# Rows of the last expert unit through a weighted one-hot product, and the overflow loop in the middle of the expert stage

## The chip, the core and the metric

The kernel runs on one core of a Trainium2 chip. Five engines work beside each other, each through its own list of instructions in order: TensorE (PE, matrix products into PSUM), VectorE (DVE), ScalarE (ACT), GpSimd (POOL) and SyncE (SP, which here issues most of the DMAs). They wait for each other by semaphores. The metric is the device time in us of one execution. Three runs of the kernel before took 1588.84 to 1589.75 us, median 1589.25 us.

## The reference

Two layers of a transformer over 512 tokens of width 1024, all in fp32. Each layer is a token mixer with four branches, which the change doesn't touch, and a mixture of experts with a residual and a layer norm:

```python
for l in range(DEPTH):
    mix = _token_mixer(x, ...)
    x = _layernorm(alpha * x + mix, ln1_g[l], ln1_b[l])
    ffn = _hier_moe(x, ...)
    x = _layernorm(alpha * x + ffn, ln2_g[l], ln2_b[l])
...
def expert_block(args):
    xe, e = args
    hid = jax.nn.silu(xe @ w_gate[e]) * (xe @ w_up[e])
    return hid @ w_down[e]
...
y = jnp.einsum('tkd,tk->td', y_assign.reshape(n_tok, TOP_K, d), weights)
```

A router sends each token to 2 of 32 experts, so there are 1024 pairs of a token and an expert (slots). Each expert has 2 MB of gate and up weights and 1 MB of down weights.

## The kernel before

The function `moe` runs the experts of a layer, `combine` adds their rows to the residual and applies the layer norm. The first four experts are taken in their own order, the others by falling number of tokens. They form 18 units of 128 rows: units 0 and 1 with two of the first experts each, units 2, 6, 10 and 14 with one expert of 128 rows, all others with two experts of 64 rows. Rows of an expert beyond these places are left to a loop (`tc.For_i` at L1604) whose number of rounds is computed on the chip; with these inputs it makes none.

A stream (`est`, class `Stream`, L201) brings the weights in loads of 1 MB: for each unit the gate and up weights of its experts, then the down weights of the unit before. A wide unit has 3 loads, a pair 6, a layer 96. SP issues a load as soon as its buffer is free and the DMA lane that it shares with the load eight places earlier has been served; 13 loads are kept ahead of the use.

For each unit u the steps are: `window` (its token columns copied out of `xs` by DVE and ACT), `gemm` (four pieces of gate and up products), `hidden` (ACT and DVE), `hidden_t` (two transposes and a copy), `down` (the down products, two evictions into a tile `ob`, one by ACT and one by DVE, and a `scatter` by POOL of the 128 rows to their slots in `ys_dram`). The code is written so that the gemm of unit u+1 stands between hidden and down of unit u. All of this is in a manual schedule: each engine gets its instructions in the order in which the code is written.

After unit 17, ACT multiplies the residual `x1` (two tiles, four times 128 tokens) by alpha. Then comes the loop, and behind it `combine`: SP loads from `ys_dram`, for each of four tiles of 128 tokens, the two rows of each token (`y`, L1698). ACT loads the table with the square root (L1694). In layer 0, ACT and DVE split two loads of the next layer's weights (`nxt`) into a high and a low part. For each tile `add` (L1644) then makes x = w1·y0 + x and x = w2·y1 + x on DVE, `stats` finds mean and variance (on ACT, or on DVE for tile 0 of layer 0 and tile 3 of layer 1) and `affine` normalizes. In layer 1 the result is stored; in layer 0 it is transposed and goes straight into the next layer's first products.

## Time and profile before

| | us |
|---|---|
| median of three runs | 1589.25 |
| the profiled execution | 1587.72 |
| its span, from the first to the last instruction | 1585.8 |
| TensorE busy in the span | 1466.5 |
| DVE busy | 719.8 |
| ACT busy | 563.2 |
| mean DMA rate over the span | 205 GB/s |

Busy times are those of instructions; the ends of matmuls are modelled, so a busy TensorE is not one at its peak. The profile page cuts the span into 40 slices of about 40 us. A timeline's row gives start and duration in us, engine (PEld is TensorE's weight load; q is an engine's sequencer, which issues DMAs), line of the kernel, operation, what it writes and reads, a count where equal instructions were merged, and in brackets how long the engine was idle before and what ended that.

### The profile page before, as it was taken

The numbers are of one execution on the slowest core, as the hardware profiler recorded it, in microseconds if no ns is written. First come the engines' busy times: TensorE is split into PE (matmuls) and PEld (weight loads), VectorE is DVE, ScalarE is ACT, GpSimd is POOL, SyncE is SP. The second block draws the span as 40 slices with busy tenths as digits, with TensorE's granted clock in tenths as the row PEclk, the third lists the DMA queues.
The fourth block names the chain that finished last, engine by engine and source line by source line (L and its number), as shares of the span: only waits on it lengthen the run. The fifth ranks groups of instructions, "written<-read, shape, count | busy, mean of one in ns | idle before, by whom it ended". The sixth has DMA issues, their size and how long they took to land. (4 is left out here: it accounts for less than half of the span.)

```text
span 1585.8 us, 17859 instructions
## 1 busy us (share of the span) xinstructions
PE 1466.5 (92%) x6552; PEld 939.5 (59%) x6552; DVE 719.8 (45%) x1386; ACT 563.2 (36%) x1001; POOL 138.4 (9%) x121
## 2 busy tenths in 40 slices
PE   7999999999999999988399999999999989999980
PEld 6766787788887433322197666767888874333220
DVE  7558875434455411110465578764443554111005
ACT  6666435333322211111346664353333222111113
POOL 0000000121004200000000000001110141000000
PEclk9999999999998999999799999999999999999996
DMA  5111122122247899999721121211232669999994
GB/s 216 66 67 67 54 93 87 47 100 93 98 193 278 346 419 421 420 420 415 302 87 54 60 93 54 100 67 67 72 121 80 248 234 397 419 421 420 420 399 174
DMA packets 54043, 324.59 MB, mean 205 GB/s; under 512 B 8641, under 2 KB 9281, under 8 KB 21953
## 3 DMA queue, kind: packets, MB, share of 16 engines
q1 hardware_dynamic: 44880, 299.54, 47.6%
q0 software_dynamic: 9072, 23.89, 4.0%
q8 instruction: 52, 0.85, 0.2%
q14 instruction: 39, 0.31, 0.1%
HBM read 306.62 MB, written 27.26 MB: 211 GB/s over the span
## 5 line engine op out<-in xcount | busy, mean ns | idle before, releaser
L149 PE MATMUL ps_mm<-xh,wh 128*128 128x512 f32 (+1 forms) x768 | 309.0, 403 | 8.7 <-ACT xh L128 8.1
L150 PE MATMUL ps_mm<-xl,wh 128*128 128x512 f32 (+1 forms) x768 | 303.4, 395 | 0.0
L151 PE MATMUL ps_mm<-xh,wl 128*128 128x512 f32 (+1 forms) x768 | 302.6, 394 | 0.0
L1451 PE MATMUL ps_mm<-er,xw 128*64 128x512 f32 (+1 forms) x1024 | 289.2, 601 | 10.4 <-DMA er<-in_w_gu_dram 7.0
L162 DVE TENSOR_TENSOR wl<-raw,wh 128x1280 fp32r<-128x1280 f32 (+2 forms) x116 | 169.7, 1467 | 146.0 <-ACT wh L128 145.7
L1451 PEld LDWEIGHTS ps_mm<-er,xw 128*64 128x64 f32 (+1 forms) x1024 | 89.5, 144 | 176.6 <-issue 142.0
L128 ACT ACTIVATE wh<-raw 128x1280 fp32r<-128x1280 f32 (+2 forms) x116 | 135.1, 1168 | 140.3 <-PE ps_mm L150 99.9
L149 PEld LDWEIGHTS ps_mm<-xh,wh 128*128 128x128 f32 (+1 forms) x768 | 144.2, 188 | 50.4 <-issue 10.1
L151 PEld LDWEIGHTS ps_mm<-xh,wl 128*128 128x128 f32 (+1 forms) x768 | 143.8, 187 | 33.8 <-issue 3.1
L1489 PE MATMUL ps_s<-er,ht 128*64 128x512 f32 (+1 forms) x512 | 144.1, 599 | 20.2 <-DMA er<-in_w_dn_dram 13.3
L150 PEld LDWEIGHTS ps_mm<-xl,wh 128*128 128x128 f32 (+1 forms) x768 | 144.2, 188 | 31.2 <-issue 2.0
L1459 DVE TENSOR_TENSOR sg<-sg,ps_mm 128x256 f32<-128x256 f32 x36 | 15.1, 420 | 256.8 <-ACT sg L128 256.8
L1489 PEld LDWEIGHTS ps_s<-er,ht 128*64 128x64 f32 (+1 forms) x512 | 44.0, 143 | 109.8 <-issue 76.3
L415 POOL TENSOR_TENSOR macc<-macc,sg 128x512 f32<-128x512 f32 x32 | 43.0, 1345 | 697.1 <-PE ps_mm L150 498.6
L128 ACT ACTIVATE sg<-ps_mm,par 128x512 f32<-128x512 f32 x64 | 44.1, 688 | 139.1 <-PE ps_mm L151 139.1
L705 DVE SCALAR_TENSOR_TENSOR cacc<-cvh,par,cacc 128x512 f32<-128x512 f32 x120 | 89.5, 746 | 1.7
L1473 DVE COPY ob<-ps_s 128x512 f32<-128x512 f32 x36 | 24.9, 692 | 132.0 <-PE ps_s L1489 132.0
L414 DVE SCALAR_TENSOR_TENSOR sg<-sg,ps_p 128x512 f32<-128x512 f32 x48 | 33.0, 687 | 105.3 <-PE ps_p L151 97.8
L1478 POOL DMA_INDIRECT ys_dram<-ob,rowi x36 | 35.2, 977 | 418.1 <-DVE xw L1439 307.6
L128 ACT ACTIVATE ht<-ps_t 128x256 f32<-128x256 f32 x36 | 13.8, 384 | 159.4 <-PE ps_t L1466 159.4
L128 ACT ACTIVATE sg<-ps_mm 128x256 f32<-128x256 f32 x36 | 13.8, 383 | 139.6 <-PE ps_mm L1451 139.6
L149 PE MATMUL ps_p<-yh,wh 128*128 128x512 f32 x128 | 51.2, 400 | 0.0
(410 smaller groups left out, 2029.1 us busy)
## 6 DMA issues: line engine op xcount, KB each, us to landing
er<-in_w_gu_dram SPq DMA_DIRECT2D x128, 1024.0 KB, 20.5
er<-in_w_dn_dram SPq DMA_DIRECT2D x64, 1024.0 KB, 20.6
raw<-in_wg_dram SPq DMA_DIRECT2D x32, 1280.0 KB, 5.5
raw<-in_wz_dram SPq DMA_DIRECT2D x12, 1024.0 KB, 4.8
raw<-in_w_o_dram SPq DMA_DIRECT2D x8, 1024.0 KB, 4.8
y<-ys_dram SPq DMA_DIRECT2D x8, 1024.0 KB, 10.1
x_dram<-r POOLq DMA_DIRECT2D x8, 512.0 KB, 3.8
x<-x_dram SPq DMA_DIRECT2D x4, 1024.0 KB, 16.8
```

Of the source, the lines that this page charges most:

```text
L128: inst = ACT.activation(out_, in_, func, **kw)
L149: PE.matmul(o, x.h, y.h, start=start, stop=False)
L150: PE.matmul(o, x.h, y.l, start=False, stop=False)
L151: PE.matmul(o, x.l, y.h, start=False, stop=stop)
L162: DVE.tensor_tensor(l, src, h, op=OP.subtract)
L414: DVE.scalar_tensor_tensor(sg, sg, 1.0, p2, op0=OP.add, op1=OP.mult)
L415: (DVE if n == 2 else POOL).tensor_tensor(macc[:, d], macc[:, d], sg, op=OP.add)
L705: DVE.scalar_tensor_tensor(cacc[c], cvh[c][:, j:j + S], w, cacc[c], op0=OP.mult, op1=OP.add)
L1451: PE.matmul(s_["p"][h], s_["X"][:, k, h], w[:, k % 4], start=k == 0, stop=k == KD - 1, skip_group_check=True)
L1473: DVE.tensor_copy(ob[:, 512:], p)
L1478: POOL.indirect_dma_start(out=ys_dram[:, :], out_offset=bass.IndirectOffsetOnAxis(ap=idx, axis=0), in_=ob, in_offset=None, bounds_check=SL ...
L1489: PE.matmul(p[h], s_["ht"][:, c, h], w[:, c, hf * 512:(hf + 1) * 512], start=c == 0, stop=c == 1, skip_group_check=True)
```

## The change

Four things change.

1. The loop for overflowing experts, now `beyond()`, stands between units 8 and 9 (`PAUSE`), outside the manual schedule. Its loads are issued by POOL and no longer by SP. The units are run by `run(2, 9)` and `run(9, 18)`, so unit 9's gemm no longer stands between hidden and down of unit 8, and unit 8's down weights come ahead of unit 9's weights in the stream.
2. After unit 4 (`MAP_AT`), `last_rows()` writes zeros to the slots of unit 17 and makes two matrices: `el` (row of unit 17 to token, with the router's weight, four blocks of 128 by 128, through eight small products) and `id` (the identity times alpha).
3. Unit 17 isn't scattered. `spread()` makes for each of four token tiles and each half of the width the sum alpha·x1 + el·ob in PSUM, with two products of 128x128 by 512: 16 in all. Tiles 2 and 3 are copied back to `x1` by ACT; for tiles 0 and 1 the first `add` reads PSUM. The scaling of `x1` by ACT is gone.
4. The loads of `y` are issued from the list `LOADS` after units 16 and 17, and no longer at the start of `combine`.

```diff
@@ -114,8 +114,9 @@
-    LOADS = {4: ("x1",), 3: ("x1", "nxt"), 2: ("nxt", "ln")}
-    LOADS_END = {4: ("x1",), 3: ("x1",), 2: ("ln",)}
+    LOADS = {4: ("x1",), 3: ("x1", "nxt"), 2: ("y", "ln", "y", "nxt", "y"), 1: ("y",)}
+    LOADS_END = {4: ("x1",), 3: ("x1",), 2: ("y", "ln", "y", "y"), 1: ("y",)}
+    PAUSE, MAP_AT = 8, 4
@@ -1354,7 +1355,24 @@
                     PE.matmul(p[:, :n], one[:, j], hv[:, w, j], start=j + w == 0, stop=j + w == 8)
             rowi = self.kp.tile([128, n], I32, name="rowi")
             DVE.tensor_scalar(rowi, p[:, :n], -1.0, NO_ROW, op0=OP.mult, op1=OP.add)
-            self.rowi = rowi
+            self.rowi, self.hone, self.low = rowi, hone, low
+
+        def last_map(self, i, w1, w2, e):
+
+            m8 = self.kp.tile([128, 2, 4], F32, name="m8", bufs=1)
+            for q, w in enumerate((w1, w2)):
+                DVE.tensor_tensor(m8[:, q], self.hone[:, q * 4:q * 4 + 4, i], w[:, :, 0], op=OP.mult)
+            DVE.tensor_scalar(self.low, self.low, -1.0, None, op0=OP.mult)
+            p = ps_t()
+            for t in range(4):
+                for q in range(2):
+                    j = q * 4 + t
+                    DVE.tensor_scalar(e[:, j], bfc[:, 4], self.low[:, j:j + 1], m8[:, q, t:t + 1], op0=OP.is_equal,
+                                      op1=OP.mult)
+                    PE.matmul(p[:, t * 128:(t + 1) * 128], e[:, j], ident, start=q == 0, stop=q == 1)
+            el = self.kp.tile([128, S], F32, name="el", bufs=1)
+            ACT.copy(el, p)
+            return el
@@ -1413,9 +1431,12 @@
         for i, u in enumerate(units):
             if i >= LEAD // 2:
                 for c in range(2):
+                    if c == 0 and i == PAUSE + 1:
+                        for r in units[i - 1]:
+                            est.add(expert(r, "w_dn", 0))
                     for r in u:
                         est.add(expert(r, "w_gu", c))
-                for r in units[i - 1] if i > LEAD // 2 else ():
+                for r in units[i - 1] if i > LEAD // 2 and i != PAUSE + 1 else ():
                     est.add(expert(r, "w_dn", 0))
         for r in units[-1]:
             est.add(expert(r, "w_dn", 0))
@@ -1489,8 +1510,33 @@
                         PE.matmul(p[h], s_["ht"][:, c, h], w[:, c, hf * 512:(hf + 1) * 512], start=c == 0, stop=c == 1,
                                   skip_group_check=True)
                 evict(ob, hf, p)
-            i = row0(units[u][0]) // CAP
-            scatter(ob, R.rowi[:, i:i + 1])
+            if u == UNITS - 1:
+                spread(ob)
+            else:
+                i = row0(units[u][0]) // CAP
+                scatter(ob, R.rowi[:, i:i + 1])
+
+        def last_rows():
+            i = row0(units[-1][0]) // CAP
+            zero = xb.tile([128, D], F32, name="ob", tag="ob", bufs=2)
+            DVE.memset(zero, 0.0)
+            scatter(zero, R.rowi[:, i:i + 1])
+            e = xb.tile([128, 8, 128], F32, name="ob", tag="ob", bufs=2)
+            st["el"] = R.last_map(i, w1, w2, e)
+            st["id"] = xb.tile([128, 128], F32, name="ida", bufs=1)
+            DVE.tensor_scalar(st["id"], ident, ALPHA, None, op0=OP.mult)
+
+        def spread(ob):
+            for t in range(4):
+                acc.append(((ps_y, ps_p), (ps_mm, ps_mm), (ps_s, ps_s), (ps_mm, ps_t))[t])
+                acc[t] = [f() for f in acc[t]]
+                x = x1[t // 2][:, t % 2]
+                for hf in range(2):
+                    o = slice(hf * 512, (hf + 1) * 512)
+                    PE.matmul(acc[t][hf], st["id"], x[:, o], start=True, stop=False)
+                    PE.matmul(acc[t][hf], st["el"][:, t * 128:(t + 1) * 128], ob[:, o], start=False, stop=True)
+                    if t > 1:
+                        table["last"] = ACT.activation(x[:, o], acc[t][hf], AF.Copy)
 
         def weigh():
             gsum = small.tile([128, 4, 1], F32, name="gsum", bufs=1)
@@ -1500,10 +1546,15 @@
             DVE.reciprocal(w1, w1)
             DVE.tensor_tensor(w2, R.d2, w1, op=OP.mult)
 
-        x1, ln = [], []
+        x1, ln, yt, acc = [], [], [], []
 
         def last_loads(name):
             if name == "nxt" and l + 1 == L:
+                return
+            if name == "y":
+                t = len(yt)
+                yt.append(ring.one((R.ep, "er2"), [128, 2, D], "y") if t < 3 else ring.last([128, 2, D], "y"))
+                SP.dma_start(yt[t], ys_dram.rearrange("(q t p) d -> t p q d", p=128, t=4)[t])
                 return
             dst = ring.last([128, 2, D], name)
             if name == "x1":
@@ -1577,70 +1628,86 @@
         ring.cycle += [(R.ep, "er2")] * 2
         est.bufs += 2
         est.limit = 1 << 30
-        window(2)
-        window(3)
+        def beyond():
+
+            nv = nc.values_load(regs[0:1, 2 * NE + 2 * OVER:2 * NE + 2 * OVER + 1], min_val=0, max_val=OVER,
+                                skip_runtime_bounds_check_because=BOUND)
+            with tc.For_i(0, nv, 1) as j:
+                v = val(bass.ds(j + 2 * NE + OVER, 1), (ENG.DVE,), SLOTS)
+                ev = val(bass.ds(j + 2 * NE, 1), (ENG.Pool,), NE - 1)
...
+                    POOL.dma_start(w.rearrange("p k n -> p (k n)"),
+                                 a["w_gu"][l][bass.ds(ev, 1), :, c * 1024:(c + 1) * 1024].rearrange("o p c -> p (o c)"))
...
+                scatter(ob, oi)
+
+        def run(lo, hi):
+            for u in range(lo, min(lo + 2, hi)):
+                window(u)
+            for c in range(4):
+                gemm(lo, c)
+            hidden(lo)
+            for u in range(lo, hi):
+                if u + 2 < hi:
+                    window(u + 2)
+                for c in range(4):
+                    if u + 1 < hi:
+                        gemm(u + 1, c)
+                    if c == 1:
+                        hidden_t(u)
+                if u + 1 < hi:
+                    hidden(u + 1)
+                down(u)
+                if u == MAP_AT:
+                    last_rows()
+                for name in (LOADS_END if l + 1 == L else LOADS).get(UNITS - u, ()):
+                    last_loads(name)
+
         weigh()
...
-        for t in range(2):
-            act(x1[t], x1[t], AF.Copy, scale=ALPHA)
+        run(2, PAUSE + 1)
         manual.__exit__(None, None, None)
-        nv = nc.values_load(regs[0:1, 2 * NE + 2 * OVER:2 * NE + 2 * OVER + 1], min_val=0, max_val=OVER,
-                            skip_runtime_bounds_check_because=BOUND)
-        with tc.For_i(0, nv, 1) as j:
-            v = val(bass.ds(j + 2 * NE + OVER, 1), (ENG.DVE,), SLOTS)
-            ev = val(bass.ds(j + 2 * NE, 1), (ENG.SP,), NE - 1)
...
-                SP.dma_start(w.rearrange("p k n -> p (k n)"),
-                             a["w_gu"][l][bass.ds(ev, 1), :, c * 1024:(c + 1) * 1024].rearrange("o p c -> p (o c)"))
...
-            scatter(ob, oi)
+        beyond()
+        manual = tc.manual_schedule()
+        manual.__enter__()
+        run(PAUSE + 1, UNITS)
+        manual.__exit__(None, None, None)
         for p in (bpool, apool, ering, spool):
             close(p)
-        return w1, w2, x1, ln[0], nxt, ring, epool
-
-    def combine(l, dst, w1, w2, xp, ln, nxt, ring, epool):
+        return w1, w2, x1, ln[0], nxt, yt, acc, ring, epool
+
+    def combine(l, dst, w1, w2, xp, ln, nxt, yt, acc, ring, epool):
         last = l == L - 1
         lng, lnb = ln[:, 0], ln[:, 1]
         x2 = [xp[t // 2][:, t % 2] for t in range(4)]
-        yt, mv, pt = [], [], {}
+        mv, pt = [], {}
         scrap = []
 
         def add(t, q):
+            if q == 0 and t < 2:
+                for hf in range(2):
+                    o = slice(hf * 512, (hf + 1) * 512)
+                    DVE.scalar_tensor_tensor(x2[t][:, o], yt[t][:, q, o], w1[:, t], acc[t][hf], op0=OP.mult, op1=OP.add)
+                return
             DVE.scalar_tensor_tensor(x2[t], yt[t][:, q], (w1, w2)[q][:, t], x2[t], op0=OP.mult, op1=OP.add)
 
         def stats(t):
@@ -1693,9 +1760,6 @@
         with tc.manual_schedule():
             pre = ACT.preload_act_table_set("sqrt_and_others")
             tc.add_manual_dep(pre.ins, table["last"].ins.name, order, reason="activation table")
-            for t in range(4):
-                yt.append(ring.last([128, 2, D], "y"))
-                SP.dma_start(yt[t], ys_dram.rearrange("(q t p) d -> t p q d", p=128, t=4)[t])
```

What this makes of the order on the engines is shown at three places. The first is SP around the loop. Before (layer 1), it stands behind all weight loads, with the loads of x1 and the layer norm's parameters just ahead of it and the y loads behind (the loop's own body is left out; DMAHW0 to 7 are the lanes of SP's DMAs, DMASW0 to 7 those of POOL's):

```order
L1515 DMA ln<-in_ln_g_dram 128x1024 [waits DMAHW0_49,PE_49]
L1516 DMA ln<-in_ln_b_dram 128x1024 [waits DMAHW1_49]
L1602 TENSOR_LOAD regs [waits DVE_49]
L1604 COMPARE_AND_BRANCH
...
L1604 UNCONDITIONAL_BRANCH [waits DMASW5_49,DMASW4_49,DMASW6_49,DMASW3_49,DMASW7_49,DMASW2_49,DMAHW0_49,DMASW1_49,DMAHW1_49,DMASW0_49,DMAHW2_49,SP_sequencer_49,DMAHW3_49,DVE_sequencer_49,DMAHW4_49,PE_sequencer_49,DMAHW5_49,Activation_se
L1698 DMA y<-ys_dram 128x2x1024 x4
```

Now the same loop stands between weight loads; the row ahead is the 61st load of the layer:

```order
L224 DMA er<-in_w_dn_dram 128x2048 [waits DMAHW4_49,PE_49]
L1633 TENSOR_LOAD regs [waits DVE_49]
L1635 COMPARE_AND_BRANCH
...
L1635 UNCONDITIONAL_BRANCH [waits DMASW5_49,DMASW4_49,DMASW6_49,DMASW3_49,DMASW7_49,DMASW2_49,DMAHW0_49,DMASW1_49,DMAHW1_49,DMASW0_49,DMAHW2_49,SP_sequencer_49,DMAHW3_49,DVE_sequencer_49,DMAHW4_49,PE_sequencer_49,DMAHW5_49,Activation_se
L1408 TENSOR_LOAD regs
L224 ISA
L224 DMA er<-in_w_gu_dram 128x2048
L1408 TENSOR_LOAD regs
L224 ISA
L224 DMA er<-in_w_gu_dram 128x2048
```

The exit (L1604 before, L1635 now) waits for all lanes in both; now it has the other 35 weight loads behind it, and the first of these carry no wait.

The second is ACT at the end of layer 0, from unit 17's copy of the transposed hidden rows. Before (the loop's body left out):

```order
L128 ACTIVATE ht<-ps_t 128x256 [waits PE_49,Activation_49]
L1475 ACTIVATE ob<-ps_s 128x512 [waits DVE_49,DMASW3_49,PE_49,Activation_49]
L128 ACTIVATE x_5383<-x_5383 128x2048 [waits DMAHW4_49,DMAHW3_49,DMAHW5_49,DMAHW2_49,DMAHW7_49,DMAHW1_49,DMAHW0_49]
L128 ACTIVATE x_5440<-x_5440 128x2048 [waits DMAHW4_49,DMAHW5_49,DMAHW3_49,DMAHW6_49,DMAHW2_49,DMAHW1_49]
L1602 TENSOR_LOAD regs [waits DVE_49]
...
L1604 UNCONDITIONAL_BRANCH [waits DMASW5_49,DMASW4_49,DMASW6_49,DMASW3_49,DMASW7_49,DMASW2_49,DMAHW0_49,DMASW1_49,DMAHW1_49,DMASW0_49,DMAHW2_49,SP_sequencer_49,DMAHW3_49,DVE_sequencer_49,DMAHW4_49,PE_sequencer_49,DMAHW5_49,Activation_se
L1694 ACT_TABLE_LOAD
L128 ACTIVATE wh<-nxt 128x1024 x4
```

Now:

```order
L129 ACTIVATE ht<-ps_t 128x256 [waits PE_49,Activation_49]
L1496 ACTIVATE ob<-ps_s 128x512 [waits DVE_49,DMASW3_49,PE_49,Activation_49]
L1539 ACTIVATE x_5544<-ps_s 128x512 [waits DMAHW2_49,DMAHW1_49,PE_49]
L1539 ACTIVATE x_5544<-ps_s 128x512 [waits PE_49]
L1539 ACTIVATE x_5544<-ps_mm 128x512 [waits PE_49]
L1539 ACTIVATE x_5544<-ps_t 128x512 [waits PE_49]
L1761 ACT_TABLE_LOAD
L129 ACTIVATE wh<-nxt 128x1024 [waits DMAHW4_49,DMAHW5_49,DMAHW3_49,DMAHW2_49]
L129 ACTIVATE wh<-nxt 128x1024
L129 ACTIVATE wh<-nxt 128x1024 [waits DMAHW7_49]
L129 ACTIVATE wh<-nxt 128x1024
```

Four copies out of PSUM (L1539) have come between the eviction of unit 17 (L1496) and the table load, in the place of the two scalings and the loop. Layer 1 has the same rows without the splits (wh).

The third is DVE behind unit 4. Before (L1459 is unit 5's hidden product, L1473 the eviction of unit 4, L1439 the window of unit 7):

```order
L1459 TENSOR_TENSOR sg<-sg,ps_mm 128x256 [waits Activation_49]
L1473 COPY ob<-ps_s 128x512 [waits DMASW6_49,DVE_49,PE_49]
L1390 TENSOR_LOAD regs
L1439 ISA
L1439 COPY xw<-xs 128x8x64 [waits DVE_49]
L1459 TENSOR_TENSOR sg<-sg,ps_mm 128x256 [waits Activation_49]
```

Now (the same are L1480, L1494 and L1460):

```order
L1480 TENSOR_TENSOR sg<-sg,ps_mm 128x256 [waits Activation_49]
L1494 COPY ob<-ps_s 128x512 [waits DMASW6_49,DVE_49,PE_49]
L1522 MEMSET ob 128x1024 [waits DMASW7_49,DVE_49]
L1364 TENSOR_TENSOR m_4670<-rhone,w_3984 128x4
L1364 TENSOR_TENSOR m_4670<-rhone,w_3985 128x4
L1365 TENSOR_SCALAR rlow<-rlow 128x8
L1370 TENSOR_SCALAR ob<-bfc,rlow,m_4670 128x128 [waits DMASW0_49,DVE_49,Activation_49]
L1370 TENSOR_SCALAR ob<-bfc,rlow,m_4670 128x128 x7
L1527 TENSOR_SCALAR ida<-cst 128x128
L1408 TENSOR_LOAD regs
L1460 ISA
L1460 COPY xw<-xs 128x8x64
```

Between the eviction of unit 4 and the window of unit 7 stand now the zeros, small products for the weights, eight one-hot tiles and the scaled identity. The first one-hot waits for DMASW0, the lane of unit 4's scatter, whose tile's buffer it takes over.

## Rows read from the trace of the kernel before

**Rows 1.** The page's 40 slices of the span: TensorE's busy tenths, its granted clock in tenths, and GB/s moved by DMA.

```profile
PE   7999999999999999988399999999999989999980
PEclk9999999999998999999799999999999999999996
GB/s 216 66 67 67 54 93 87 47 100 93 98 193 278 346 419 421 420 420 415 302 87 54 60 93 54 100 67 67 72 121 80 248 234 397 419 421 420 420 399 174
```

**Rows 2.** Stretches by window: from:to, length, then busy time (and instructions) of PE, PEld, DVE, ACT and POOL, the granted clock as a share of full speed, the DMA share and GB/s. The first two are of layer 0's expert stage, the others of its end and the next layer's start.

```profile
577.26:631.38 54.12, 54.12 (x225) 18.57 (x226) 7.24 (x15) 9.29 (x20) 4.87 (x5) 1.00 1.01 420
665.88:764.22 98.34, 86.83 (x304) 27.38 (x302) 9.46 (x20) 13.78 (x28) 6.81 (x7) 1.00 1.00 414
764.22:774.00 9.78, 0.00 (x0) 0.00 (x0) 0.70 (x2) 2.89 (x3) 0.97 (x1) 0.77 0.24 91
774.00:787.28 13.28, 0.00 (x0) 0.00 (x0) 10.89 (x14) 5.11 (x6) 1.18 (x2) 0.50 0.97 392
791.00:796.70 5.70, 5.64 (x26) 5.64 (x27) 5.24 (x8) 2.13 (x5) 0.00 (x0) 0.50 0.04 14
796.70:800.00 3.30, 3.30 (x30) 3.30 (x29) 2.90 (x4) 2.98 (x5) 0.00 (x0) 0.99 0.40 159
```

**Rows 3.** The timeline at the end of layer 0's expert stage: unit 16's scatter, then from unit 17's down products on.

```profile
758.14 0.97 POOL L1478 DMA_INDIRECT ys_dram<-ob,rowi  x1 [14.63 <-ACT ht L128]
...
760.53 0.20 PEld L1489 LDWEIGHTS ps_s<-er,ht 128*64 128x64 f32 x4 [2.78 <-SPq L1604]
...
762.55 0.60 ACT L1475 ACTIVATE ob<-ps_s 128x512 f32<-128x512 f32 x1 [5.04 <-PE ps_s L1489]
763.04 3.70 ACT L128 ACTIVATE x<-x 128x2048 f32<-128x2048 f32 x2
...
764.22 0.69 DVE L1473 COPY ob<-ps_s 128x512 f32<-128x512 f32 x1 [6.83 <-PE ps_s L1489]
766.57 0.97 POOL L1478 DMA_INDIRECT ys_dram<-ob,rowi  x1 [7.46 <-DMA ys_dram<-ob,rowi]
773.49 7.55 SPq L1698 DMA_DIRECT2D y<-ys_dram  x4
773.63 1.28 ACT L1694 ACT_TABLE_LOAD   x1 [6.89 <-issue]
774.93 3.90 ACT L128 ACTIVATE wh<-nxt 128x1024 fp32r<-128x1024 f32 x4
776.02 4.63 DVE L162 TENSOR_TENSOR wl<-nxt,wh 128x1024 fp32r<-128x1024 f32 x4 [1.89 <-ACT wh L128]
780.57 2.60 DVE L1644 SCALAR_TENSOR_TENSOR x<-y,w,x 128x1024 f32<-128x1024 f32 x2
```

**Rows 4.** The timeline at the end of layer 1, and (the last two rows) the chain of work that ended last, in order of time, with the duration of each piece.

```profile
1549.38 0.69 DVE L1473 COPY ob<-ps_s 128x512 f32<-128x512 f32 x1 [6.84 <-PE ps_s L1489]
...
1562.45 1.06 ACT L128 ACTIVATE scrap<-x 128x1024 f32<-128x1024 f32 x1 [6.91 <-DVE x L1644]
...
1582.06 0.99 SPq L1669 DMA_DIRECT2D out_dram<-x  x2
...
1550.82 2.27 DMA ys_dram<-ob,rowi
...
1553.88 5.90 DMA y<-ys_dram
```

**Rows 5.** The timeline of SP at one place, and the DMA issues by tile from 646 to 762 us, with count, size and median us from issue to landing.

```profile
644.51 0.33 SPq L223 DMA_DIRECT2D er<-in_w_dn_dram  x1
...
er<-in_w_gu_dram SPq DMA_DIRECT2D x22, 1024.0 KB, 21.0
er<-in_w_dn_dram SPq DMA_DIRECT2D x13, 1024.0 KB, 21.4
```

**Rows 6.** The timeline of TensorE's weight loads: the first of unit 4's and of unit 9's gate and up products, and of unit 10's down products.

```profile
577.26 0.20 PEld L1451 LDWEIGHTS ps_mm<-er,xw 128*64 128x64 f32 x4 [0.76 <-issue]
...
631.38 0.14 PEld L1451 LDWEIGHTS ps_mm<-er,xw 128*64 128x64 f32 x2 [0.29 <-issue]
...
666.52 0.30 PEld L1489 LDWEIGHTS ps_s<-er,ht 128*128 128x128 f32 x2 [0.81 <-issue]
```

**Rows 7.** The timeline of layer 0's expert stage: a window copy, and half of a wide unit's gate and up products, four fp32 products 128x128 by 512 (two instructions each).

```profile
700.10 0.61 ACT L1439 COPY xw<-xs 128x512 f32 x1
701.17 3.70 PE L1451 MATMUL ps_mm<-er,xw 128*128 128x512 f32 x8
```

**Rows 8.** DMA issues of the whole span, with count, size and median us to landing: loads of 1 MB in the mixer, where the queue is short, and the scatters.

```profile
raw<-in_wz_dram SPq DMA_DIRECT2D x12, 1024.0 KB, 4.8
...
ys_dram<-ob,rowi POOLq DMA_INDIRECT x36, 8.4
```

**Rows 9.** The timeline of ACT around a table load in layer 0's mixer.

```profile
132.58 0.60 ACT L128 ACTIVATE at<-ps_s 128x512 f32<-128x512 f32 x1 [0.96 <-PE ps_s L459]
133.20 1.28 ACT L135 ACT_TABLE_LOAD   x1
134.49 1.20 ACT L128 ACTIVATE qh<-ps_mm 64x512 f32<-64x512 f32 x2
```

60 lines of the change are left out of this document (22 added, 38 removed).

## The prediction

> **What bounds the kernel now.** I read the page first for the shape. Of the span of 1585.8 us the two expert stages are the stretches in which the GB/s line stands at about 420, slices 15 to 19 and 35 to 39 [rows 1]. The stretches by window say what limits them. From 577.26 to 631.38 TensorE is busy all the time and DMA too, so TensorE is still working off a backlog. From 665.88 to 764.22 TensorE is busy for 86.8 of 98.3 us while DMA stays full at 414 GB/s [rows 2]. So the second half of the stage is bound by the weight stream, and TensorE has some 12% in hand, no more.
>
> Then the end of each stage. In layer 0 TensorE finishes at 764.22, where DVE starts the last eviction. The last scatter goes out at 766.57, the y loads at 773.49, ScalarE changes its table at 773.63 and splits the next layer's weights, and the first add comes at 780.57: 16.35 us after TensorE's end [rows 3]. In layer 1 TensorE ends at 1549.38 and ScalarE's first statistic starts at 1562.45, 13.07 us later; behind that the rest runs as one chain of DVE work to the last store at 1582.06 [rows 4]. These two tails are what the change rewrites.
>
> **Part 1: the loop in the middle.** Before, the skipped loop stood behind all weight loads. Now it stands behind unit 8. The order of SP shows what it costs to pass it even with no round to run: the exit waits for every DMA lane, and the first two loads behind it wait for nothing, because by then all lanes are empty. The other engines hold the same wait at their exit, TensorE among them. So everything issued before must land, and nothing is issued meanwhile.
>
> How much is that? Units 0 to 8 need 48 loads of 1 MB (12 + 3 + 18 + 3 + 12), and the stream counts 14 buffers by then and keeps 13 loads ahead, so 61 loads stand before the loop and 35 behind it. In the trace of before the 61st load is the single w_dn load that SP issues at 644.51; 22 + 13 = 35 follow it [rows 5]. With 21 us to landing that is about 665.6, and indeed TensorE's use of it starts at 666.52 [rows 5, 6]. In the changed kernel the stream up to there is fed as before, so I keep 665.6 as the end of the drain.
>
> From there TensorE has nine units to do. Its price for a unit without waiting is read where it had a backlog: the starts at 577.26 and 631.38 are five units apart, 54.12 / 5 = 10.82 us each [rows 6]. Nine units take 97.4 us. Ahead of them come the exit (in layer 1's chain 0.8 us pass from the landing of the scatter at 1553.09, that is 1550.82 + 2.27, to the y load at 1553.88 [rows 4]), a register load and a window copy (0.61 [rows 7]); no row shows the sum, so I take 2.5, between 1.4 and 4. The last unit has nothing to cover its hidden chain: 1.0. TensorE will have been idle for some 15 to 20 us. After 10 us without work its granted clock was at 0.50, the lower of the two levels, and 5.7 us of dense work still ran at 0.50 before it was back at 0.99 [rows 2]; that costs 2.8. Sum: 665.6 + 2.5 + 97.4 + 1.0 + 2.8 = 769.3, against 764.2: +5.1 a layer.
>
> The stream gives the same answer by itself. A load that finds the queue empty takes 4.8 us and not the 2.5 us that 1 MB takes at 420 GB/s [rows 8]: with the exit a gap of about 3. The third load needs the buffers of the first half unit of unit 9, free only at about 8.5 us; it lands near 13.3, where the second had landed near 8: another gap of about 3. Both bounds are tight, and each now waits at times for the other, so I take +6 a layer, **+12** in all. It can't be below nothing, since the stream ran full in this stretch before and carries the same loads; the upper end is under the rivals.
>
> **Part 2: the map and the zero rows after unit 4.** The tile for the one-hot rows takes the buffer of unit 4's output, and in the order DVE's first one-hot waits for the lane of that scatter, which lands 8.4 us after issue [rows 8]. Behind this instruction DVE holds the window copy and TensorE its eight one-hot products and all of unit 6's work. A scatter goes out about 2 us after its unit's last matmul (764.22 to 766.57 [rows 3]); with eight small instructions on DVE and TensorE each, 2 + 8.4 + 1.5, TensorE loses about 12 us. I cost this at nothing, because it ends before the drain does: unit 8's transposes and down products stand at the place of unit 9's start, 631.38 [rows 6], and with some 4.5 us TensorE would reach the loop at 636, with the pause at 648, well before 665.6, and the loads have 21 us to landing where 4.8 would do [rows 5, 8], so the stream survives a pause of 12. If that cover is gone, it costs up to 12 us a layer.
>
> **Part 3: the end of a layer.** Gone are the last scatter, the loop and the wait for y. In their place TensorE makes 16 fp32 products 128x128 by 512. Four such take 3.7 us with their start, or 0.86 apart [rows 7]: 13.7 us, beginning where the last down matmul ends. The stretch is dense, so full clock. The first output tile is complete after 3.4 us, and if DVE's add were next, this would be a gain of 7 us a layer. But ScalarE takes tiles 2 and 3 out of PSUM, and the order puts these four copies ahead of its table load and everything behind it. The last one can start when the last product is done: 13.7 + 0.6 (the same shape as the eviction at 762.55 [rows 3]) + 1.28 for the table + 0.1 of handing over = 15.7 us after TensorE's end.
>
> Layer 1: the first statistic at 15.7 and not at 13.07, and the chain behind it is unchanged (the second tile's adds, which were hidden under it, stay hidden): **+2.6**. Layer 0: behind the table come the splits of the next weights, and DVE's adds stand behind those in its order. From the first split at 774.93 to the last DVE part at 776.02 + 4.63 = 780.65 it was 5.7 us [rows 3], so the add comes at 21.4 instead of 16.35: **+5.1**. The y loads are not what ends the wait: the first goes out when unit 16's scatter (758.14 [rows 3]) has landed, 8.4 us later and so about 2 us behind TensorE's end, and is there at 2 + 4.8, about 7; behind it come ln, y, nxt and two more y, 2.5 us for each MB, the last at about 20.
>
> The table load is 1.28 us, and in the trace one that follows directly on ScalarE work is followed directly by the next: 133.18, 133.20 to 134.48, 134.49 [rows 9]. The Trainium skill (ScalarE: Activation LUTs, What ACT_TABLE_LOAD costs) puts about 1.38 us of drain on top of the 1.28 us, 2.66 us for each change of set, and such a drain would speak against a table load that now stands right behind ScalarE's copies. By that rule the sum would be 2.8 us higher, an estimate from the page; the trace does not agree.
>
> ScalarE's two scalings of x (1.85 us each [rows 3]) go, and were hidden.
>
> **The sum.** 12 + 2.6 + 5.1 = 19.7 us. The profiled execution took 1587.72 us, so 1607.4; the median shown is 1.5 us above it: 1609.
>
> **Rivals.**
> - The drain costs nothing, since the restart finds a full ring and TensorE's 12% are enough: only the tails remain, 1589.25 + 7.7 = 1597. For it: 13 loads lie ready. Against: nine units at 10.82 fill the 98.3 us by themselves. Chance 0.10.
> - The pause at unit 4 reaches the stream, because buffers come free too late: up to 12 us a layer more, 1621 to 1633. For it: at that point SP waited for TensorE's buffers, too. Against: the 21 us to landing. Chance 0.08.
> - The tail is won, the other side: ScalarE's table load and first statistic run before its copies of tiles 2 and 3. Then layer 1's statistic starts at 3.4 + 0.7 + 1.3 = 5.4 and gains 7.6, and layer 0's add starts when y is there and the splits are done, at about 8, and gains 8: 1589.25 - 15.6 = 1573.6 without a drain cost, 1585.6 with it. It decides from the point where the first statistic starts before the last product ends. The order speaks against it. Chance 0.07.
> - The losses and gains cancel, 1589: chance 0.03.
>
> **How the numbers follow.** The forecast has 0.72. A measurement of this kernel can tell 0.2%, about 3.2 us, from no change. Slower holds the forecast and the first two rivals, less a little for values near the bound: 0.88. Same 0.05, faster 0.07. The range for 8 in 10 goes from 1596, just under the first rival, to 1624, into the second: what is left out is both cases below and the worse half of the second.
>
> **What would show it.** In the profile after: a stretch without TensorE work before about 665 and again before 1451, ended by a DMA, with DMA at full rate almost to its end and then a dip; the half clock at the restart; TensorE nearly without waits for weights behind it; a TensorE pause of about 12 us after unit 4; 16 products of 0.86 us after the last down; ScalarE's table load right behind the copies. I am wrong if DMA shows no dip, if the first statistic comes before the last product, or if the pause after unit 4 shows in the GB/s.

## The result and the profile after

The changed kernel took 1609.63 us (median of 4 runs, 1608.72 to 1613.21) against 1589.41 for the kernel before: ratio 1.0139, interval 1.0128 to 1.0151. It is slower, by 20.2 us from median to median; 1609 had been forecast. The two medians make a ratio of 1.0127, just under that interval, and the ratio given would make 22 us. The profiled execution has a span of 1607.1 us (before 1585.8).

The page's slices of the changed kernel, as in [rows 1]:

```profile
PE   7999999999999888599599999999999989795993
...
PEclk9999999999998998799899999999999999997997
...
GB/s 217 61 66 79 43 102 86 60 72 116 87 239 233 395 420 419 315 415 412 308 86 53 54 97 53 98 66 66 92 119 59 276 229 416 421 416 345 417 387 183
```

Each expert stage now has one slice in which the GB/s line falls out of its plateau: 315 in layer 0, 345 in layer 1. The stretches by window of layer 0 (columns as in [rows 2]) show what lies there:

```profile
599.00:612.27 13.27, 3.55 (x16) 3.58 (x17) 3.80 (x15) 0.00 (x0) 1.94 (x2) 0.62 1.01 420
612.27:649.70 37.43, 36.89 (x145) 12.72 (x144) 3.67 (x7) 6.70 (x14) 2.90 (x3) 1.00 1.01 418
649.70:669.09 19.39, 0.00 (x0) 0.00 (x0) 1.12 (x2) 0.69 (x2) 0.97 (x1) 0.59 0.63 261
669.09:673.40 4.31, 4.31 (x10) 1.23 (x12) 0.43 (x1) 0.46 (x1) 0.00 (x0) 0.50 0.92 310
673.40:690.00 16.60, 16.60 (x62) 6.12 (x60) 1.82 (x4) 2.88 (x6) 0.00 (x0) 0.99 0.95 382
690.00:764.00 74.00, 74.00 (x310) 25.14 (x308) 9.23 (x20) 11.52 (x25) 6.80 (x7) 1.00 1.01 412
```

In the first, TensorE pauses at unit 4 while DMA stays at 420 GB/s. In the third it does nothing for 19.39 us and DMA moves 261 GB/s on average. Then come 4.31 us at a granted clock of 0.50 (1.2 GHz), and from 690 on TensorE is busy all the time. Before, it was busy for 86.8 of the last 98.3 us [rows 2]; that reserve is used up.

The third stretch in pieces, from 656 on, up to the restart:

```profile
656.00:659.00 3.00, 0.00 (x0) 0.00 (x0) 0.00 (x0) 0.00 (x0) 0.97 (x1) 0.50 1.02 423
659.00:662.00 3.00, 0.00 (x0) 0.00 (x0) 0.00 (x0) 0.00 (x0) 0.00 (x0) 0.50 0.74 302
662.00:665.00 3.00, 0.00 (x0) 0.00 (x0) 0.00 (x0) 0.00 (x0) 0.00 (x0) 0.50 0.17 67
665.00:667.43 2.43, 0.00 (x0) 0.00 (x0) 0.00 (x0) 0.00 (x0) 0.00 (x0) 0.50 0.05 20
667.43:669.09 1.66, 0.00 (x0) 0.00 (x0) 0.43 (x1) 0.69 (x2) 0.00 (x0) 0.50 0.00 0
```

DMA is full until 659 and then runs out over 8.4 us, long before the last load of the drain has landed (667.43). Against 421 GB/s it moves 2.4 MB less in these 8.4 us, 5.7 us of its rate. What keeps the last bytes back so long is not shown.

The timeline of the changed kernel at the same places: the wait of DVE and TensorE behind unit 4; SP's 61st and 62nd weight loads and TensorE's restart; the end of layer 0; the end of layer 1.

```profile
608.23 2.21 DVE L1370 TENSOR_SCALAR ob<-bfc,rlow,m 128x128 f32<-128x128 bf16 x8 [7.95 <-DMA ys_dram<-ob,rowi]
608.72 3.75 PE L1372 MATMUL ps_t<-cst,ob 128*128 128x128 f32 x16 [10.44 <-DVE ob L1370]
...
646.08 0.33 SPq L224 DMA_DIRECT2D er<-in_w_dn_dram  x1
668.41 7.86 SPq L224 DMA_DIRECT2D er<-in_w_gu_dram  x4
...
669.09 13.04 PE L1472 MATMUL ps_mm<-er,xw 128*64 128x512 f32 x40 [19.39 <-SPq L1408]
...
772.30 0.69 DVE L1494 COPY ob<-ps_s 128x512 f32<-128x512 f32 x1 [5.58 <-PE ps_s L1510]
...
786.23 0.60 ACT L1539 ACTIVATE x<-ps_t 128x512 f32<-128x512 f32 x1 [1.12 <-PE ps_t L1537]
786.84 1.28 ACT L1761 ACT_TABLE_LOAD   x1
788.14 3.95 ACT L129 ACTIVATE wh<-nxt 128x1024 fp32r<-128x1024 f32 x4
...
789.23 4.63 DVE L163 TENSOR_TENSOR wl<-nxt,wh 128x1024 fp32r<-128x1024 f32 x4 [16.24 <-ACT wh L129]
793.78 0.74 DVE L1709 SCALAR_TENSOR_TENSOR x<-y,w,ps_y 128x512 f32<-128x512 f32 x1
...
1567.77 0.69 DVE L1494 COPY ob<-ps_s 128x512 f32<-128x512 f32 x1 [5.64 <-PE ps_s L1510]
...
1581.70 0.60 ACT L1539 ACTIVATE x<-ps_t 128x512 f32<-128x512 f32 x1 [1.12 <-PE ps_t L1537]
1582.31 1.28 ACT L1761 ACT_TABLE_LOAD   x1
1583.61 1.06 ACT L129 ACTIVATE scrap<-x 128x1024 f32<-128x1024 f32 x1
```

SP issues nothing between 646.08 and 668.41. The 61st load lands 21.35 us after its issue, at 667.43, and 1.66 us later TensorE starts. Layer 0's first add stands at 793.78, 21.5 us behind TensorE's end (16.35 before [rows 3]); layer 1's first statistic at 1583.61, 15.8 us behind it (13.07 before [rows 4]). In both layers ScalarE's table load follows directly on the last of its four copies.

The 61st load is where the forecast's sum for the loop starts, so here is its way in all four stages: to landing in layer 0 before (issued at 644.51 [rows 5]) and after, then issue and time to landing in layer 1 before and after.

```profile
er<-in_w_dn_dram SPq DMA_DIRECT2D x1, 1024.0 KB, 21.3
er<-in_w_dn_dram SPq DMA_DIRECT2D x1, 1024.0 KB, 21.4
...
1430.01 0.33 SPq L223 DMA_DIRECT2D er<-in_w_dn_dram  x1
er<-in_w_dn_dram SPq DMA_DIRECT2D x1, 1024.0 KB, 21.0
...
1444.69 0.33 SPq L224 DMA_DIRECT2D er<-in_w_dn_dram  x1
er<-in_w_dn_dram SPq DMA_DIRECT2D x1, 1024.0 KB, 18.3
```

Before, it landed at 665.85 and 1451.02, 98.4 us ahead of TensorE's end in both layers. Now it lands at 667.43 and 1462.97, 104.9 and 104.8 us ahead of it: 6.5 and 6.4 us more.

So that runs can be compared, the span is cut at four marks: a layer's first expert weight load on SP, the last eviction of unit 17 on DVE, the next layer's first weight load, and the span's last instruction. Before, these pieces are 304.3 us (stage of layer 0), 482.1 (its end and the next mixer), 303.0 (stage of layer 1) and 36.4 (its end). The table gives what each run's profiled execution has more or less than that, in us, and its ratio to the kernel before over all runs. Each kernel has one profiled execution. The stages of e5, which has no loop, differ from those before by 1.1 us either way, and the stretch ahead of the first mark, which no edit touches, by up to 2.0 us: smaller differences say nothing.

| run | stage 0 | end 0 | stage 1 | end 1 | ratio, interval |
|---|---|---|---|---|---|
| changed kernel | +7.8 | +5.7 | +4.6 | +3.0 | 1.0139, 1.0128 to 1.0151 |
| e1 no loop, cut kept | +4.0 | +3.9 | -0.8 | +2.9 | 1.0070, 1.0048 to 1.0093 |
| e3 one-hot rows apart | +6.0 | +5.9 | +5.3 | +2.9 | 1.0130, 1.0113 to 1.0147 |
| e4 no copies | +8.5 | +6.9 | +4.4 | -2.8 | 1.0113, 1.0094 to 1.0132 |
| e5 new end alone | +1.1 | +4.6 | -1.1 | +2.9 | 1.0057, 1.0040 to 1.0074 |
| e6 end freed, no loop | -0.9 | +3.0 | +2.7 | -6.1 | 1.0000, 0.9990 to 1.0010 |
| e7 loop moved, alone | +5.3 | -0.6 | +4.6 | -0.1 | 1.0054, 1.0037 to 1.0070 |
| e8 loop before unit 2 | +10.7 | +3.4 | +9.6 | -5.9 | 1.0112, 1.0095 to 1.0129 |
| e9 loop in unit 17 | +14.4 | -5.3 | +11.7 | -6.4 | 1.0075, 1.0058 to 1.0092 |
| e10 loop behind unit 12 | +18.1 | -0.6 | +14.7 | -1.2 | 1.0194, 1.0177 to 1.0211 |
| e11 loop behind unit 4 | +4.2 | -0.6 | +4.5 | -1.4 | 1.0063, 1.0043 to 1.0083 |
| e12 loop before the spread | +1.0 | +4.0 | -0.8 | -0.4 | 1.0025, 1.0014 to 1.0037 |

The changed kernel's four pieces make 21.1 of the 21.3 us by which its span grew.

### The profile page after: what moved, and what is told of

Read it like the earlier page. It is cut to its first block, busy times and chain, and to the rows that moved or that the text cites. A ratio compares the mean times of both kernels' runs of the same rounds, so it can differ in the third digit from the quotient of the medians.

```text
span 1607.1 us, 18064 instructions
## 1 busy us (share of the span) xinstructions
PE 1473.0 (92%) x6648; PEld 954.2 (59%) x6648; DVE 727.5 (45%) x1416; ACT 562.5 (35%) x1007; POOL 138.4 (9%) x122
## 5 line engine op out<-in xcount | busy, mean ns | idle before, releaser
L1472 PE MATMUL ps_mm<-er,xw 128*64 128x512 f32 (+1 forms) x1024 | 265.9, 606 | 39.9 <-SPq L1408 19.4
L1510 PE MATMUL ps_s<-er,ht 128*64 128x512 f32 (+1 forms) x512 | 133.3, 597 | 4.3 <-ACT ht L129 2.1
L1480 DVE TENSOR_TENSOR sg<-sg,ps_mm 128x256 f32<-128x256 f32 x36 | 15.1, 420 | 236.0 <-ACT sg L129 236.0
L1494 DVE COPY ob<-ps_s 128x512 f32<-128x512 f32 x36 | 24.9, 691 | 108.2 <-PE ps_s L1510 108.2
```

Of the source, the lines that this page charges most:

```text
L1472: PE.matmul(s_["p"][h], s_["X"][:, k, h], w[:, k % 4], start=k == 0, stop=k == KD - 1, skip_group_check=True)
L1494: DVE.tensor_copy(ob[:, 512:], p)
L1510: PE.matmul(p[h], s_["ht"][:, c, h], w[:, c, hf * 512:(hf + 1) * 512], start=c == 0, stop=c == 1, skip_group_check=True)
```

## The experiments

The theory: the loop's exit drains every transfer and costs 12 to 13 us, ScalarE's copies at the end cost 8, the pause at unit 4 is covered. Against it: the cut of the pipeline into two pieces costs, not the drain; the pause costs; or the 16 products, not the copies, set the end.

**e1: the loop out, the cut kept.**

```diff
         run(2, PAUSE + 1)
         manual.__exit__(None, None, None)
-        beyond()
         manual = tc.manual_schedule()
```

> The skipped loop for overflowing experts is left out, and nothing stands in its place; units 2 to 8 and 9 to 17 still run as two pieces, and the map stays after unit 4. If it is the drain at the loop's exit that costs the 8.1 and 4.6 us by which TensorE's end moved, they come back but for what the cut pipeline costs, 0 to 3 us: 1597 to 1600 us. If it is the cut into two pieces that costs, nothing comes back: 1606 us or more. If the pause of 13 us at unit 4 is part of the cost, it now has no cover and eats the gain: 1602 to 1610 us.

Measured: 1597.34 us, with 1587.21 for the kernel before beside it. By the ratios 0.7% of the time is left of 1.4%: some 11 us came back. In the 40 us from 655 on DMA is full again (420 GB/s) and TensorE never idle. From the 61st load's landing to TensorE's end e1 takes 100.6 and 99.0 us, 98.4 before. Of the first, 1.65 us are a granted clock of 0.50 (763 to 765) at unit 17's last 14 down products, which take 3.65 us in e5, where the clock stays at 1.00:

```profile
763.02 5.30 PE L1510 MATMUL ps_s<-er,ht 128*64 128x512 f32 x14 [1.90 <-DMA er<-in_w_dn_dram]
```

The drain it is, then; for the cut, together with the pause at unit 4 that e1 keeps, 0.6 us a layer are left, no more than executions differ by. The rest of the +4.0 in layer 0's stage is a 61st load that landed 1.7 us later in its stage than before; in e5, which has neither cut nor pause nor loop, it is 1.1 us later.

**e7: the loop's move alone,** with the old end of the layer, no loop there, and no map after unit 4. The cut into two pieces stays.

```diff
-            if u == UNITS - 1:
-                spread(ob)
-            else:
-                i = row0(units[u][0]) // CAP
-                scatter(ob, R.rowi[:, i:i + 1])
+            i = row0(units[u][0]) // CAP
+            scatter(ob, R.rowi[:, i:i + 1])
```

> The move of the loop alone: it stands behind unit 8 as in the changed kernel, and the end of the layer is that of the kernel before (scatter of the last unit, y loads, scaling of x), without a loop there. If the drain costs 8.1 and 4.6 us and the tails the other 8, this gives 1589.4 + 12.7, less 0 to 4 us for the loop that no longer stands ahead of the y loads: 1598 to 1602 us. If the drain costs nothing by itself and it is the pause at unit 4 that made TensorE late, 1586 to 1591 us.

Measured: 1596.48, +9.3 us: the size of the middle loop by itself, a little under the lower end. The whole of it lies in the stages, +5.3 and +4.6; the ends stand as before, so the loop had cost little where it was: without it there, these pieces are shorter by 0.1 to 1.4 us in e7, e10 and e11. What the stream lost is seen in a window of 40 us from 655 on, first of this run, then of the kernel before:

```profile
655.00:695.00 40.00, 26.60 (x96) 9.20 (x98) 3.15 (x7) 4.41 (x9) 0.98 (x1) 0.77 0.81 321
```

```profile
655.00:695.00 40.00, 36.48 (x133) 11.62 (x130) 3.92 (x8) 5.12 (x11) 2.92 (x3) 1.00 1.02 421
```

At 100 GB/s less over 40 us, 4 MB weren't moved: 9.5 us at 421 GB/s. The stage lost about half of that, and the landings say why the bytes mislead: counted from the stage's first load, the loads behind the hole land some 5 us later than before, the last of them 5.3 us in layer 0 and 4.6 in layer 1, as much as the stages lost. From the 61st load's landing to TensorE's end e7 takes 104.4 us in both layers, 6.0 more than before.

**e3: the one-hot rows in tiles of their own.**

```diff
-                    DVE.tensor_scalar(e[:, j], bfc[:, 4], ...
+                    e = self.kp.tile([128, 128], F32, name="ea", bufs=3)
+                    DVE.tensor_scalar(e, bfc[:, 4], ...
```

> The one-hot rows go to small tiles of their own instead of the buffer of unit 4's output, so that DVE doesn't wait there for the scatter; the loop stays. If the drain covers the pause, TensorE only reaches the loop earlier and waits longer: 1608 to 1610 us, the same within 0.1%. If the pause reaches the stream through late buffers, the landing of the 61st load, and with it the restart, comes 1.5 to 12 us earlier in each layer: 1600 us or less in the clear case.

Measured: 1608.37, the ratio 1.0130 against 1.0139 with intervals that overlap. TensorE is done with unit 5 some 9 us earlier, counted from the stage's first load, and waits longer at the loop. The pause at unit 4 is covered; the stages show +6.0 against +7.8 in layer 0 and +5.3 against +4.6 in layer 1, about the scatter of one execution, and from the 61st load's landing to TensorE's end 105.0 and 105.4 us, no less than with the pause (104.9 and 104.8).

The cover is thin, though. The exit waits for unit 8's scatter too, which goes out only when unit 7's has landed; first that row of the changed kernel, then the waits of SP at its exit, both layers together (total, times, longest):

```profile
657.05 0.97 POOL L1499 DMA_INDIRECT ys_dram<-ob,rowi  x1 [9.42 <-DMA ys_dram<-ob,rowi]
...
SPq L1635 <- DMA ys_dram<-ob,rowi: 34.9, 2, 18.1
SPq L1635 <- DMA er<-in_w_dn_dram: 2.1, 2, 1.9
```

The 61st load comes behind the scatter by 1.9 us in layer 0 and by 0.2 us in layer 1. In e4, below, no wait for the load is left behind the scatter's, and the next weight load goes out 1.6 us after the 61st has landed, not 1.0 as here: there the scatter ended the drain.

**e10 and e11: the move alone, behind unit 12 and behind unit 4.**

```diff
-    PAUSE, MAP_AT = 8, 4
+    PAUSE, MAP_AT = 12, 4
```

(The other has 4 in place of 12; no map is made in these two.)

> The move of the loop alone, as in the run with that move, but behind unit 12 instead of unit 8; the end of the layer is that of the kernel before. If a layer's loss is the later of two bounds (TensorE's remaining units at 10.8 us each from the landing of the last load ahead of the loop, or the stream's refill), the 85th load decides, which landed at 728.7 in layer 0 before: 728.7 + 1.7 + 5 x 10.82 + 1.0 + 2.4 = 787.9 against 764.2, some 20 to 24 us a layer: 1626 to 1636 us. If passing the loop has one price wherever it stands, 1596 to 1600 us as behind unit 8.

> The same, behind unit 4: 37 loads stand ahead of the loop, the last of them landed at 600.5 in layer 0 before, when TensorE gets there. TensorE then has 603 + 13 x 10.82 = 744 to its end if it never waits, 20 us in hand. If only TensorE's idle time counts, nothing is lost: 1587 to 1590 us. If the stream's refill counts too (behind unit 8 it moved 4 MB less than before in the 40 us around the restart, 9.5 us of its rate), the loss is 4 to 9 us a layer: 1596 to 1606 us.

Measured: 1619.17 (+30.4) and 1598.4 (+9.6), beside 1588.81. One price wherever the loop stands is refuted: behind unit 12 it costs three times as much. TensorE's restarts, first behind unit 12, then behind unit 4, there with its waits up to the end of the stage (total, times, longest):

```profile
724.66 13.64 PE L1472 MATMUL ps_mm<-er,xw 128*64 128x512 f32 x40 [31.90 <-DVE xw L1460]
```

```profile
610.07 13.38 PE L1472 MATMUL ps_mm<-er,xw 128*64 128x512 f32 x40 [17.50 <-ACT xw L1460]
```

```profile
PE ps_s L1510 <- DMA er<-in_w_dn_dram: 4.8, 3, 1.9
PE ps_mm L1472 <- DMA er<-in_w_gu_dram: 1.7, 2, 1.3
```

Behind unit 12 TensorE is the bound: from 724.66 to the last eviction at 783.50 are 58.8 us for five units, 54.1 by the price of a unit, the rest the slow clock and the bare hidden chain. Behind unit 4 it would have been through at 610.07 + 13 x 10.82 + 3.4 = 754 and ends at 770.47, with waits for weights on the way: there the stream's hole is the bound, and costs 4.2 and 4.5 us. Both halves of the theory hold. My counts of the loads ahead were off: 82 and not 85 stand ahead of the later loop, 40 and not 37 ahead of the earlier one, so the one landed at 722.7 (728.7 expected), the other at 608.7 (600.5). That is most of the miss in the first figure.

**e4: DVE adds all four tiles out of PSUM.**

```diff
-                    if t > 1:
-                        table["last"] = ACT.activation(x[:, o], acc[t][hf], AF.Copy)
...
-            if q == 0 and t < 2:
+            if q == 0:
```

> ScalarE's four copies of tiles 2 and 3 go: DVE adds all four tiles straight out of PSUM (the tiles change places in PSUM for that). If the copies ahead of the table load are what the tail costs, layer 1's first statistic comes 6 to 7 us after TensorE's last down product instead of 15.8, and layer 0's first add 16 to 17 instead of 21.5, where the load of the next layer's second weight then ends the wait: 9 + 5 us less, 1594 to 1598 us. If the 16 products or the y loads set the tail, the first statistic stays at 13 us or later: 1604 to 1610 us.

Measured: 1605.52, 1.0113: by the ratios some 4 us came back, not 14. The timeline, layer 0 and then layer 1:

```profile
787.47 2.36 DVE L163 TENSOR_TENSOR wl<-nxt,wh 128x1024 fp32r<-128x1024 f32 x2 [13.30 <-PE ps_t L1537]
...
791.87 2.00 ACT L129 ACTIVATE wh<-nxt 128x1024 fp32r<-128x1024 f32 x2 [14.45 <-DMA nxt<-in_w_foxv_dram]
...
1569.96 0.69 DVE L1494 COPY ob<-ps_s 128x512 f32<-128x512 f32 x1 [5.94 <-PE ps_s L1510]
...
1577.06 1.06 ACT L129 ACTIVATE scrap<-x 128x1024 f32<-128x1024 f32 x1 [6.86 <-DVE x L1709]
```

In layer 1 the statistic comes 7.1 us behind TensorE's end, as expected for the copies; but the second tile's y lands only 10 us behind it (DVE's next add waits for it until 1579.96), so the last store gains 5.8 and not 9. In layer 0 nothing is gained: DVE's low parts wait for the last product (787.47; that they are written where the spread's operands lay is read from the code), and the second weight of the next layer, queued behind y, lands only at 791.87. The copies were one of three things that ended there together.

**e5: the new end alone** (no loop, one piece, one-hot rows apart).

```diff
-        run(2, PAUSE + 1)
...
-        beyond()
...
-        run(PAUSE + 1, UNITS)
+        run(2, UNITS)
```

> The changed end of the layer alone: the skipped loop is left out, units 2 to 17 run in one piece as in the kernel before, and the one-hot rows have tiles of their own. Compared with the first of these runs it takes away the cut and the pause at unit 4 as well. If the tails cost 5.2 and 2.8 us and all else came from the loop, the cut and the pause, this is 1587.2 + 8 = 1594 to 1596.5 us on this chip. If what was left there (10.1 us above the kernel before) came from the tails alone, it stays at 1597 us or more; if the tails cost nothing by themselves, 1587 to 1590 us.

Measured: 1596.41, +8.1 us, all of it in the ends: +4.6 and +2.9 in the pieces. Together with the 9.3 of the loop's move this is 17.4 of the 20.2 us; the rest, up to 3, no run has by itself.

**e6: the end freed of what came late.** As e5, with e4's adds, the next layer's weight and ln loaded ahead of y, and the low parts behind the first tile:

```diff
-    LOADS = {4: ("x1",), 3: ("x1", "nxt"), 2: ("y", "ln", "y", "nxt", "y"), 1: ("y",)}
+    LOADS = {4: ("x1",), 3: ("x1", "nxt"), 2: ("nxt", "ln", "y", "y", "y"), 1: ("y",)}
...
                         columns(0)
+                        for lo, src, h in lows_:
+                            DVE.tensor_tensor(lo, src, h, op=OP.subtract)
```

> As the run with the changed end alone (the skipped loop is left out, one piece, one-hot rows apart), and the end freed of what came late: DVE adds all four tiles out of PSUM; the load of the next layer's second weight goes ahead of y, ln too; and DVE's low parts of that weight stand behind the first tile's add, statistic and scaling, since in the run with the tail freed they waited for the last product. If it was ScalarE's copies and then that order, layer 0's first add comes 7 to 9 us after TensorE's end (16.4 before the change), layer 1's first statistic at 6 to 7 (13.1): 1578 to 1584 us, faster than the kernel before. If the 16 products bound the end whatever stands behind them, 1590 us or more.

Measured: 1587.9 against 1588.33, ratio 1.0000: the 8 us of the end are gone, but the 1578 to 1584 us that had been expected are missed; a gain over the kernel before is not there. Layer 1's end is 6.1 us shorter. Layer 0's is still 3 longer, by two rows:

```profile
779.67 1.41 DVE L1702 SCALAR_TENSOR_TENSOR x<-y,w,ps_s 128x512 f32<-128x512 f32 x2 [14.08 <-DMA y<-ys_dram]
...
796.31 0.56 PE L150 MATMUL ps_mm<-wh,xh 128*128 128x256 f32 x1 [7.81 <-DVE x L1702]
```

The first y was issued at 766.54 and landed 12.9 us later (4.8 in e12, where the queue had been drained); and the next layer's first products wait for a PSUM bank that the third tile's add gives back. Of the +2.7 in layer 1's stage 1.7 are the clock: unit 17's last 14 down products took 5.34 us and not the 3.65 of e5, behind a wait as short as there (1.91 us, 1.89 in e5), at the granted clock of this row:

```profile
1552.00:1553.80 1.80, 1.80 (x6) 0.48 (x4) 0.00 (x0) 0.13 (x1) 0.00 (x0) 0.50 0.14 55
```

**e8, e9, e12: whole kernels, with the loop at three other places,** each with an end like e6's.

```diff
+                if u == UNITS - 1:
+                    manual.__exit__(None, None, None)
+                    beyond()
+                    manual = tc.manual_schedule()
+                    manual.__enter__()
                 down(u)
```

(This is e9, in unit 17 ahead of its down products. In e8 the same four lines stand ahead of `run(2, UNITS)`, before unit 2, and in e12 ahead of `spread(ob)`.)

> The same freed end, with the loop in it, ahead of unit 2, where the stream has only its first loads to drain: nothing of the computation is left out. If a drain costs what TensorE and the stream can't make up behind it, and here it is short, 0 to 4 us a layer over the run without a loop: 1578 to 1590 us. If a drain costs a refill of the stream wherever it stands, 8 to 13 us over it: 1588 to 1596 us.

> The same freed end, with the loop between the hidden rows and the down products of the last unit: the weights that it waits for are needed there anyway, and the y loads stand behind it. Nothing of the computation is left out. If the drain then waits only for the scatter of unit 16 (some 2 to 4 us beyond the last weights), TensorE ends 4 to 7 us later than without a loop, y lands some 5 us behind the exit, and the sum is 1582 to 1590 us. If the exit costs a refill or a slow clock that counts here, 1591 us or more.

> Nothing of the computation is left out: the loop stands where it was before, behind the last unit's down products and ahead of the product that spreads them; y is loaded behind it, DVE adds all tiles out of PSUM, with banks that the next layer's first products don't wait for, and one-hot rows apart. If a drain costs nothing where all that it waits for is due anyway, and the spread runs while y is on its way, it saves the last scatter (up to 2.5 us in layer 1, up to 6 in layer 0 if y then lands earlier): 1580 to 1588 us. If in layer 0 the transfers ahead of y fill the queue until then anyway, and the 16 products end later than y lands, 1588 to 1594 us.

Measured: 1605.45, 1600.04 and 1592.66, beside 1588.33 (the first two) and 1588.81. None beats the kernel before. e9 and e12 lie in the worse of their two ranges, e8 above both: early the loop is dear, not cheap; the stretch in question by window, e8 and then e6, which has no loop:

```profile
550.00:570.00 20.00, 13.25 (x49) 6.18 (x48) 4.50 (x12) 3.51 (x6) 2.00 (x2) 0.74 0.58 226
```

```profile
550.00:570.00 20.00, 17.55 (x74) 7.59 (x74) 5.28 (x14) 4.64 (x9) 2.00 (x2) 1.00 1.01 420
```

194 GB/s less over 20 us are 3.9 MB, or 9.2 us. What ends this drain is no load. The last one ahead of the loop, the 20th, lands at 556.65; but the exit waits for unit 1's scatter, which goes out only at 557.63, and SP issues the next load only at 562.12, 5.5 us after the 20th has landed (1.0 behind unit 8). First SP's longest wait at the exit, both layers together, then the two rows:

```profile
SPq L1633 <- DMA ys_dram<-ob,rowi: 32.1, 2, 17.1
...
557.63 0.99 POOL L1500 DMA_INDIRECT ys_dram<-ob,rowi  x1 [5.40 <-DVE w L1544]
562.12 2.04 SPq L224 DMA_DIRECT2D er<-in_w_gu_dram  x3
```

From there on, counted from the stage's first load, the loads land 9.0 to 10.7 us later than before in layer 0, and 7.1 to 7.9 in layer 1; the rest of that stage's 9.6 is the clock, as in e6 (unit 17's last 14 down products take 5.34 us). In e9 TensorE waits at the loop, and in e12 too, in both for a load that it has no use for:

```profile
773.76 6.03 PE L1511 MATMUL ps_s<-er,ht 128*64 128x512 f32 x16 [14.84 <-DMA ln<-in_ln_b_dram]
```

```profile
773.11 2.08 PE L1541 MATMUL ps_s<-x,ida 128*128 128x512 f32 x2 [6.64 <-DMA ln<-in_ln_b_dram]
```

My expectation for e9 had counted the scatter and the weights, not x, the next layer's weights and ln, which SP had issued just ahead of the loop.

## Why the prediction was right

The sum was 19.7 us and the measurement is 20.2 from median to median; its terms, one by one:

- **The loop, +12.** Counted from the landing of the 61st load to TensorE's end, as the forecast counted, a layer takes 6.5 and 6.4 us more than before, and 6.0 in e7, for a forecast of 6. The steps in layer 0: the load landed at 667.43 (forecast 665.6), TensorE restarted 1.66 us later (2.5), and from 669.09 to 772.30 it took 103.2 us (97.4 + 1.0 + 2.8 = 101.2). Half of the 4.31 us at 0.50, 2.2, is the cost of the clock (2.8 forecast). These steps alone had made +5.1; that it was rounded up to 6 rested on no row, and that 6 fits better is luck. By whole stages the layers look unlike, +7.8 and +4.6, because the load landed 1.3 us later in layer 0's stage than before and 1.8 us earlier in layer 1's; e5, with no loop, differs there by +1.1 and -2.4. In e7 the load landed 0.7 and 1.5 us earlier than before, so that its stages show 9.9 us and its time 9.3; taken as time, 12 lies just above the end of e7's interval (1.0070, some 11 us).
- **The stream's side of it.** The forecast had two gaps of about 3 us in the stream, both behind the landing, and DMA at full rate almost to its end. The second did not come so: DMA falls off 8.4 us ahead of the landing, and 5.7 us of its rate are lost there (4.6 of the 9.5 in e7), which the forecast did not have. Counted from the 61st load, the last load of a layer lands 6.5 us later than before (6.0 in e7), near the forecast's 6 all the same. Behind the restart TensorE waits 0.8 us for weights; that engine and stream bind about equally there is argued from e10 and e11 on either side, not shown by a run of its own.
- **The pause at unit 4, 12 us, at nothing.** TensorE's work on unit 6 began at 612.27, where 598.9 stood before (577.26 and two units of 10.82 [rows 6]): 13.4 us. The GB/s stayed at 420, and e3 gives no difference that can be measured. The rival in which the pause reaches the stream falls, but for at most 2 us in layer 0. TensorE reached the loop at 649.7, forecast 648. The reason given was not whole: the forecast compared TensorE's arrival with the landing of the load and left out unit 8's scatter, which lands only 1.9 and 0.2 us ahead of the load, where the forecast had some 17 us to spare. That the pause stayed covered was close.
- **The ends, +5.1 and +2.6.** 21.5 us against a forecast of 21.4 in layer 0, 15.8 against 15.7 in layer 1; +5.7 and +3.0 in the pieces, 8.1 in e5's time. The sizes are right. The reason was whole only for layer 1: in layer 0 the copies came late, but had they not, the low parts would have waited for the last product and the next layer's weight (e4). The step "ScalarE's copies ahead of its table load" named one of the late ones as if it were the only one.
- **The table load:** 786.23 + 0.60, then 786.84 + 1.28, then 788.14: no drain beside it, as the row of before said and the Trainium skill (ScalarE: Activation LUTs, What ACT_TABLE_LOAD costs) did not.
- **The rivals.** A drain that costs nothing is refuted by e1 and e7. The won tail was priced too high: freed of the copies, and without a loop, e6 comes back to the kernel before, not to 15.6 us under it. Layer 1's end gained 6.1 of the rival's 7.6 us; layer 0's lost 3 where the rival had a gain of 8, with y 12.9 us on its way behind the next weights and a PSUM bank that came free late.

## What to carry to other kernels

A loop that runs no round was still, in this kernel, a point at which every transfer in flight must land, those that nobody waits for too, and at which no new one is issued. At every place inside the stream of weights it cost more than behind it, however idle the engines were. Price it from the landing of the last transfer ahead of it, once with the engine's remaining work and once with the transfers that are not made meanwhile, and take the later. That last transfer need not be a load: look for the scatter of the unit just done. And count landings rather than bytes: a hole of 9.5 us in bytes (e7) moved the landings by 5 to 6. When a late engine is to be taken off an end, list all that ends there within a few us before counting the gain.
